# Loads, an operand sum and feed-forward buffers placed anew in a one-core encoder block

## The chip, the cores and the metric

The kernel runs on one core of a Trainium2 chip. The metric is the device time of one execution in microseconds; the time before is the median of three runs. All engine times below come from one profiled execution of the kernel before.

## The reference

One layer over x of 2048 tokens by 1024 features, all in float32:

```python
h = rms_norm(x, pre_mix_g)
proj = h @ w_in                      # attention q/k/v, RWKV r/k/v + low rank, two gates
y_a = chunk_band_attention(q, k, v, rel_bias)
y_b = rwkv7_time_mix(p_rwkv, ...)
merged = gate_a * (y_a @ proj_a) + gate_b * (y_b @ proj_b)
x = x + rms_norm(merged @ w_out, post_mix_g)
hf = rms_norm(x, pre_ffn_g)
u = square(relu(hf @ w_up)) @ w_down # w_up 1024 x 4096, w_down 4096 x 1024
x = x + rms_norm(u, post_ffn_g)
```

`rms_norm` divides a row by the root of its mean square and multiplies by a gain.

## The kernel before, in words

**Number format.** Each float32 operand of a large product is split into a rounded high part and the rest (`split`, lines 69 to 71: a cast on ScalarE, ACT in the profile, then a subtraction on VectorE, DVE). A product is three matmuls (`mm3`, line 73): high by high, high by low, low by high. Nearly every large operand therefore passes through ACT and DVE before TensorE (PE) may use it.

**Mixing.** The 2048 tokens are worked on in four groups (g = 0 to 3) of 512. For each group `run` (line 1378) calls `phase_rwkv`, `phase_attention` and `phase_merge`. At the end of `phase_attention` eight blocks of branch B (y_b @ proj_b, times its gate) are computed by `branch` (line 1007) and stored in DRAM as md. `phase_merge` (line 1019) then does:

- for i in 0 to 7 the branch-A block: loads mb (md, line 1031), th (the gate, line 1011) and wraw (proj_a, line 1013), 256 KB each; 12 matmuls into ps_p; then th is multiplied, mb added and the sum split into mh and ml. The blocks where i is above 2 also advance the generator `beside` by one step.
- the output projection, in two halves n of 512 columns. Each half has eight blocks k: a w_out load of 256 KB, a split, and 12 matmuls into ps_o (four token tiles by three). In the second half, after blocks 0, 2, 4 and 6, the generator `between` is advanced by one step.

**`beside`** is one of twenty operand sums (`combine`, line 1087) for the feed-forward part, which needs sums and differences of blocks of its operands: four loads of 256 KB into cmb, four DVE subtractions in place, each a step of the generator and kept in program order on DVE, and four stores. Loads and stores go through GpSimd's queue (POOL). One such sum belongs to each merge; `run` takes its first step, the loads, just before `phase_merge`.

**`between`** is the norm of the next group's input, `phase_norm` (line 282): it loads the gain g_pre (512 KB) and for each of four token tiles loads x (512 KB) through SyncE's queue (SP), squares and sums it on ACT, makes the root on POOL, multiplies on DVE (line 298), and transposes it in eight matmuls (`transpose_split`, line 118; pstr), with a cast and a subtraction for each four.

**Order.** A planner places the traced instructions on each engine's queue by its own timing model. A ready instruction can so come ahead of those traced before it. Each engine runs its queue in order. `keep_in_program_order` pins an instruction behind the one traced before it on its engine; `queue_behind(a, b)` (line 83) places a behind b on a queue without waiting for b to finish. In the trace the transposes of the first token tile stand ahead of most of the output projection.

**Feed-forward part.** Two halves of two groups each. `phase_up` (line 1140) computes seven combinations of the hidden layer for sixteen pairs of blocks: five or seven products (ps_u) per pair, with operands from w_up (wraw split by `parts` into a1, s12, s3, s4) and from the combined h (tiles t4, b22, t2, t3, t1, each high and low). For the first eight pairs the first two products are made ahead, with the buffers a1, s12, s3 in turn. The hidden values pass `hidden` (an addition, Relu, Square) and go to DRAM as xd. `phase_down` (line 1258) runs 56 steps s; each loads an xd block and a w_down (or combined wd) block of 512 KB, splits both into one operand tile fop (16 KB in each partition; `operands`, line 1282), and does 24 matmuls into ps_dn. Operands are made two steps ahead. `final` (line 1324) adds up squares, normalizes, adds the residual and stores.

**Memory.** Pools on the left grow up, those with side="right" grow down, both as a stack: a pool opened later lies further in, over whatever an earlier closed pool had there. With reuse_waits="tile" a tile waits only for the tiles whose bytes it takes. The pools raw (four 4 KB tiles), cb and z (two 16 KB buffers) live through the whole feed-forward part; z holds the tiles z and X in the up phase and fop in the down phase.

Of the kernel before, what the change touches and what calls it, by code (L numbers as in the profile page):

```python
# [18 lines left out]
P = 128  # L19
D = 1024  # L20
# [30 lines left out]
class Block:  # L51
# [17 lines left out]
    def split(self, hi, lo, src):  # L69
        self.nc.scalar.copy(hi, src)  # L70
        self.nc.vector.tensor_tensor(lo, src, hi.bitcast(F32), ALU.subtract)  # L71

# [45 lines left out]
    def transpose_split(self, pt, src, hi, lo, tok):  # L118

        nc = self.nc  # L120
        for h in range(2):
            ps = pt.tile([P, 4, P], F32, tag="tr", name="pstr")
            for j in range(4):
                k = h * 4 + j
                nc.tensor.transpose(ps[:, j], src[:, k * P : (k + 1) * P], self.ident)
# [166 lines left out]
    def norm_tile(self, sp, pt, x, gt, hi, lo, tok, ahead=2):  # L292
# [6 lines left out]
        self.transpose_split(pt, xn, hi, lo, tok)  # L299
# [719 lines left out]
    def phase_merge(self, g, o, op, between, beside):  # L1019

        tc, nc, a = self.tc, self.nc, self.a
        with ExitStack() as ctx:
# [6 lines left out]
            for i in range(KB):  # L1029
# [5 lines left out]
                if i > 2:  # L1035
                    advance(beside, 1)
            self.yctx.close()
            for n in range(2):
                ps = [po.tile([P, 512], F32, tag="o", name="ps_o") for _ in range(GT)]
                for k in range(KB):  # L1040
# [7 lines left out]
                    if n == 1 and k % 2 == 0:  # L1048
                        advance(between, 1)
# [51 lines left out]
    def combinations(self, half):  # L1101
# [4 lines left out]
        for k in range(KH):  # L1106
            src = (g0[:, k], g1[:, k], g0[:, KH + k], g1[:, KH + k])
            yield lambda b, src=src, k=k: self.combine(
                b, lambda i, t: dma(t, src[i]), lambda i, t: dma(self.td[half][:, i, k], t)
            )  # L1110

    def down_combinations(self):
# [3 lines left out]
        for i in range(FF // P // 2):  # L1116
            yield lambda b, i=i: self.combine(
                b, lambda c, t: dma(t, rows[i, c // 2, c % 2]), lambda c, t: dma(self.wd[c][i // 2][:, i % 2], t)
            )

# [19 lines left out]
    def phase_up(self, half, zp, rp, cb, pn, early):  # L1140
# [6 lines left out]
        with ExitStack() as ctx:  # L1147
            e = ctx.enter_context
            tb = e(tc.tile_pool(name="ht", bufs=1, reuse_waits="tile"))
            up = e(tc.tile_pool(name="up", bufs=1, reuse_waits="tile"))  # L1150
            sp = e(tc.tile_pool(name="ops", bufs=1, side="right", reuse_waits="tile"))
            bh, bl = self.b1
            B11, B21 = (bh[:, lo4], bl[:, lo4]), (bh[:, hi4], bl[:, hi4])
            z = zp.tile([P, early, G], F32, tag="z", name="z")
            X = zp.tile([P, 7, G], F32, tag="z", name="X")
            T = {
                n: [tb.tile([P, KH, G], F32R, name=n + x) for x in "hl"] for n in ("t4", "b22", "t2", "t3", "t1")
# [24 lines left out]
            def parts(src, tag, n):  # L1182
                hl = [sp.tile([P, n, P], F32R, tag=tag + x, name=tag + x) for x in "hl"]
# [74 lines left out]
    def phase_down(self, half, zp, rp, cb, pn, beside_of):  # L1258
# [213 lines left out]
```

## Time and profile before

| | us |
|---|---|
| median of three runs | 3354.83 (3352.9 to 3360.96) |
| the profiled execution | 3351.23 |
| its span in the profile | 3349.5 |
| PE busy | 3205.5 (96%) |
| DVE busy | 2245.0 (67%) |
| ACT busy | 1581.6 (47%) |
| POOL busy | 605.0 (18%) |
| DMA over the span | 592.56 MB, mean 177 GB/s |

The profiled execution's time holds the span and what lies around it. Rows of the timeline read: start, duration, engine, line, operation, tile written <- tiles read, shapes, count, and in brackets how long the engine was idle before and what ended that. SPq and POOLq are the queues that issue DMAs. A row of the windows reads: stretch, its length, busy time of the engine with its instructions in parentheses, the granted TensorE clock, the share of the 16 DMA engines' time, GB/s. PEld rows are TensorE's weight loads, which overlap its matmuls.

### The profile page before, as it was taken

The page shows a single profiled execution, that of the slowest core. Times are in us where ns is not written, and L with a number is a line of the kernel's source. Part 1 is how long each engine was busy: PE and PEld are TensorE (multiplying, and loading weights), DVE is VectorE, ACT ScalarE, POOL GpSimd, SP SyncE. Part 2 cuts the span into 40 slices and gives each one's busy share as a digit, 9 for nine tenths or more (in the row PEclk, how much of TensorE's full clock was granted, in tenths as well). Part 3 has the DMA queues.
Part 4 walks back from the last instruction along what each step waited for, and adds up shares of the span by engine and source line. Part 5 has one row for each costly group of instructions (what it writes and reads, how often), then busy time and mean ns, then how long its engine had stood idle before and what let it go on. Part 6 is the DMA issues. An engine that isn't in the chain of part 4 may idle for free. (4 is left out here: it accounts for less than half of the span.)

```text
span 3349.5 us, 50328 instructions
## 1 busy us (share of the span) xinstructions
PE 3205.5 (96%) x18913; PEld 2602.6 (78%) x18913; DVE 2245.0 (67%) x3719; ACT 1581.6 (47%) x2575; POOL 605.0 (18%) x1109
## 2 busy tenths in 40 slices
PE   7999989999989999999999999999999999999998
PEld 5777768777878777777777787878788878787887
DVE  5775666786765875765876765777655757774465
ACT  3434634444644434654444654544543444454333
POOL 2222012222111222111222110122211112210000
PEclk9999999999999999999999999999999999999999
DMA  5335374247464236655326647654777875546665
GB/s 150 89 117 188 112 227 125 79 139 241 152 227 139 88 109 221 196 178 176 95 77 200 199 138 239 232 179 161 253 259 245 291 228 190 167 160 225 195 211 180
DMA packets 448668, 592.56 MB, mean 177 GB/s; under 512 B 26324, under 2 KB 313248, under 8 KB 448424
## 3 DMA queue, kind: packets, MB, share of 16 engines
q1 hardware_dynamic: 390184, 408.94, 39.4%
q0 software_dynamic: 49024, 163.61, 13.6%
q10 hardware_dynamic: 9216, 16.78, 1.4%
q8 instruction: 149, 2.44, 0.3%
q14 instruction: 95, 0.78, 0.1%
HBM read 425.37 MB, written 167.01 MB: 177 GB/s over the span
## 5 line engine op out<-in xcount | busy, mean ns | idle before, releaser
L1307 PE MATMUL ps_dn<-fop 128*128 128x512 f32 x2688 | 614.6, 390 | 8.6 <-ACT fop L70 5.2
L1307 PEld LDWEIGHTS ps_dn<-fop 128*128 128x128 f32 x2688 | 505.6, 188 | 115.6 <-ACT fop L70 6.1
L79 PE MATMUL psd<-hh,whi 128*128 128x512 f32 x1344 | 539.3, 401 | 10.0 <-ACT whi L70 7.5
L79 PE MATMUL psd<-hh,wlo 128*128 128x512 f32 x1344 | 538.2, 400 | 2.7 <-DVE wlo L71 2.6
L79 PE MATMUL psd<-hl,whi 128*128 128x512 f32 x1344 | 539.8, 402 | 0.0
L70 ACT CAST whi<-wraw 128x1024 fp32r<-128x1024 f32 (+1 forms) x296 | 255.6, 864 | 546.5 <-PE psd L79 328.2
L71 DVE TENSOR_TENSOR wlo<-wraw,whi 128x1024 fp32r<-128x1024 f32 (+1 forms) x296 | 292.6, 989 | 238.5 <-ACT whi L70 206.2
L79 PEld LDWEIGHTS psd<-hh,whi 128*128 128x128 f32 x1344 | 255.1, 190 | 61.1 <-ACT whi L70 8.3
L79 PEld LDWEIGHTS psd<-hh,wlo 128*128 128x128 f32 x1344 | 255.1, 190 | 54.9 <-DVE wlo L71 5.2
L79 PEld LDWEIGHTS psd<-hl,whi 128*128 128x128 f32 x1344 | 255.0, 190 | 49.0
L71 DVE TENSOR_TENSOR fop<-xraw,fop 128x1024 fp32r<-128x1024 f32 x112 | 137.1, 1224 | 182.7 <-ACT fop L70 182.0
L70 ACT CAST fop<-xraw 128x1024 fp32r<-128x1024 f32 x112 | 117.7, 1051 | 262.8 <-PE ps_dn L1307 204.3
L1194 POOL DMA_DIRECT2D xd<-X x192 | 103.8, 541 | 395.2 <-ACT X L1191 341.0
L71 DVE TENSOR_TENSOR fop<-wdraw,fop 128x1024 fp32r<-128x1024 f32 x112 | 136.6, 1220 | 19.8 <-ACT fop L70 19.3
L70 ACT CAST fop<-wdraw 128x1024 fp32r<-128x1024 f32 x112 | 117.6, 1050 | 31.3 <-DMA wdraw<-in_w_down_dram 22.4
L880 DVE CUSTOM_DVE_ANT_0 sc<-bias,ps_s 128x640 f32<-128x640 f32 (+4 forms) x128 | 93.9, 734 | 55.9 <-PE ps_pt L891 39.6
L79 PE MATMUL ps_p<-yh,whi 128*128 128x512 f32 x256 | 103.4, 410 | 17.1 <-ACT whi L70 16.8
L70 ACT CAST s12h<-s 128x1024 fp32r<-128x1024 f32 x32 | 33.7, 1054 | 166.5 <-PE ps_u L79 166.5
L896 DVE TENSOR_TENSOR PTl<-ps_pt,PTh 128x640 fp32r<-128x640 f32 (+4 forms) x128 | 94.4, 738 | 26.4 <-ACT PTh L895 25.7
L885 ACT ACTIVATE sc<-sc,mn 128x640 f32<-128x640 f32 (+4 forms) x128 | 97.6, 763 | 26.8 <-DVE mn L880 26.5
L895 ACT CAST PTh<-ps_pt 128x640 fp32r<-128x640 f32 (+4 forms) x128 | 79.9, 624 | 52.8 <-PE ps_pt L891 50.4
L79 PE MATMUL ps_p<-yh,wlo 128*128 128x512 f32 x256 | 103.8, 406 | 1.0 <-DVE wlo L71 1.0
(368 smaller groups left out, 6861.5 us busy)
## 6 DMA issues: line engine op xcount, KB each, us to landing
wraw<-in_w_in_dram SPq DMA_DIRECT2D x168, 512.0 KB
xraw<-xd SPq DMA_DIRECT2D x112, 512.0 KB
xd<-X POOLq DMA_DIRECT2D x192, 256.0 KB, 5.1
wraw<-in_w_up_dram SPq DMA_DIRECT2D x80, 512.0 KB
wdraw<-wd SPq DMA_DIRECT2D x64, 512.0 KB
wdraw<-in_w_down_dram SPq DMA_DIRECT2D x48, 512.0 KB
gd<-gate ACTq DMA_DIRECT2D x64, 256.0 KB
cmb<-in_w_down_dram POOLq DMA_DIRECT2D x64, 256.0 KB, 4.4
```

Of the source, the lines that this page charges most:

```text
L70: self.nc.scalar.copy(hi, src)
L71: self.nc.vector.tensor_tensor(lo, src, hi.bitcast(F32), ALU.subtract)
L79: mm.append(nc.tensor.matmul(ps, l, r, start=n == 0, stop=n == last).ins)
L880: nc.vector.tensor_tensor_reduce(sc[:, 0:n], bias[:, s0:640], pss[:, c0 : c0 + n], 1.0, 3.0e38, ALU.add, ALU.min, mn,)
L885: nc.scalar.activation(sc[:, 0:n], sc[:, 0:n], AF.Exp, scale=-1.0, bias=mn, accum_out=sm[:, col : col + 1])
L895: nc.scalar.copy(hv, pst[:, 0:nk])
L896: nc.vector.tensor_tensor(lv, pst[:, 0:nk], hv.bitcast(F32), ALU.subtract)
L1194: nc.gpsimd.dma_start(self.xd[q][i // 2][:, i % 2], src)
L1307: nc.tensor.matmul(ps, o[:, l, k, sl], o[:, r, k], start=start and n == 0, stop=stop and n == end)
```

## The change

In the merge:

- The operand sum's five steps move from the branch loop and from before it into the first half of the output projection, after blocks 0 (loads), 3, 4, 5 and 6 (subtractions, then stores). The loads go through SP's queue instead of POOL's and are pinned there.
- The next group's norm is a new generator, `next_norm`. Its first step, after block 2 of the first half, loads the first x tile, the gain and the second x tile, pinned on SP's queue. Its four other steps come after blocks 0, 2, 4 and 6 of the second half as before; the first transpose of each four is now pinned on PE's queue. x tiles 2 and 3 are loaded right behind the steps of tiles 0 and 1, pinned too.

In the feed-forward part:

- `phase_up` has a second pool on the right, ops2, for s3 and s4 and a pad of 512 bytes; a1 and s12 stay in ops. The order of the tiles t1 and t2 in their pool is exchanged.
- In `phase_down` the pool ffo (x, gain, small tiles) is opened before ffb and ring instead of after them, with a small pad; in the second half, where ffb has nothing to hold, it gets a pad of 20,992 bytes.
- fop tiles alternate between z and ring with each step, instead of two steps in z and two in ring.
- The last Relu of the up phase is queued behind the second cast of step 1's operand on ACT.

The diff, cut where a description above says it all:

```diff
     def split(self, hi, lo, src):
-        self.nc.scalar.copy(hi, src)
+        high = self.nc.scalar.copy(hi, src)
         self.nc.vector.tensor_tensor(lo, src, hi.bitcast(F32), ALU.subtract)
+        return high.ins
...
-    def transpose_split(self, pt, src, hi, lo, tok):
+    def transpose_split(self, pt, src, hi, lo, tok, pinned=False):
...
-                nc.tensor.transpose(ps[:, j], src[:, k * P : (k + 1) * P], self.ident)
+                mm = nc.tensor.transpose(ps[:, j], src[:, k * P : (k + 1) * P], self.ident)
+                if pinned and j == 0:
+                    self.tc.keep_in_program_order(mm)
...
+    def next_norm(self, g, sp, pt):
+
+        pin, dma = self.tc.keep_in_program_order, self.nc.sync.dma_start
+        gt, xs = sp.tile([P, D], F32, tag="gain", bufs=1, name="g_pre"), []
+
+        def load(t):
+            xs.append(sp.tile([P, D], F32, tag="x", bufs=2, name="x"))
+            pin(dma(xs[-1], self.a["x"][g * G + t * P : g * G + (t + 1) * P]))
+
+        load(0)
+        pin(dma(gt, self.a["pre_mix_g"][None, :].to_broadcast((P, D))))
+        load(1)
+        yield
+        self.h = self.alloc_h()
+        for t in range(GT):
+            self.norm_tile(sp, pt, xs[t], gt, *self.h, slice(t * P, (t + 1) * P), 2, True)
+            if t + 2 < GT:
+                load(t + 2)
+            yield
...
                 self.split(mh[:, i], ml[:, i], t)
-                if i > 2:
-                    advance(beside, 1)
...
-                    if n == 1 and k % 2 == 0:
+                    if n == 0 and k in (0, 3, 4, 5, 6):
+                        advance(beside, 1)
+                    if n == 0 and k == 2 or n == 1 and k % 2 == 0:
                         advance(between, 1)
...
+    def load_in_order(self, dst, src):
+        self.tc.keep_in_program_order(self.nc.sync.dma_start(dst, src))
...
+            late = e(tc.tile_pool(name="ops2", bufs=1, side="right", reuse_waits="tile"))
             sp = e(tc.tile_pool(name="ops", bufs=1, side="right", reuse_waits="tile"))
...
+            late.tile([P, 128], F32, tag="pad", bufs=1, name="pad")
...
-                n: [...] for n in ("t4", "b22", "t2", "t3", "t1")
+                n: [...] for n in ("t4", "b22", "t1", "t3", "t2")
...
-                hl = [sp.tile([P, n, P], F32R, tag=tag + x, name=tag + x) for x in "hl"]
+                pool = sp if tag in ("a1", "s12") else late
+                hl = [pool.tile([P, n, P], F32R, tag=tag + x, name=tag + x) for x in "hl"]
...
-                nc.scalar.activation(dst, dst, AF.Relu)
+                self.relu = nc.scalar.activation(dst, dst, AF.Relu).ins
...
+            op = e(tc.tile_pool(name="ffo", bufs=2, side="right", reuse_waits="tile"))
             bp = e(tc.tile_pool(name="ffb", bufs=2, side="right", reuse_waits="tile"))
             ring = e(tc.tile_pool(name="ring", bufs=2, side="right", reuse_waits="tile"))
-            op = e(tc.tile_pool(name="ffo", bufs=2, side="right", reuse_waits="tile"))
...
+            op.tile([P, 32], F32, tag="pad", bufs=1, name="pad")
+            if half:
+                bp.tile([P, 5248], F32, tag="pad", bufs=1, name="pad")
...
-                t = (zp, ring)[s % 4 // 2].tile([P, 4, 2, G], F32R, tag=("z", "op")[s % 4 // 2], name="fop")
+                t = (zp, ring)[s % 2].tile([P, 4, 2, G], F32R, tag=("z", "op")[s % 2], name="fop")
...
-                self.split(t[:, 2], t[:, 3], wr)
+                high = self.split(t[:, 2], t[:, 3], wr)
+                if s == 1:
+                    self.queue_behind(self.relu, high)
...
-                    beside = next(sums)([b[:, i] for i in range(4)])
-                    advance(beside, 1)
-                    self.phase_merge(g, o, op, self.phase_norm(g + 1, sp, pt) if g + 1 < self.NG else iter(()), beside)
+                    beside = next(sums)([b[:, i] for i in range(4)], self.load_in_order)
+                    self.phase_merge(g, o, op, self.next_norm(g + 1, sp, pt) if g + 1 < self.NG else iter(()), beside)
```

The two generators that make operand sums take the load function as an argument (`get=dma`), so that only the sum beside a merge loads through SP.

More of the change, by code (lines that the diff above doesn't have):

```diff
@@ L290, in phase_norm, with norm_tile @@
             yield
-    def norm_tile(self, sp, pt, x, gt, hi, lo, tok, ahead=2):
+    def next_norm(self, g, sp, pt):
[14 more added lines that the diff above has]
+            yield
+    def norm_tile(self, sp, pt, x, gt, hi, lo, tok, ahead=2, pinned=False):
         nc = self.nc
@@ L298, in norm_tile @@
         nc.vector.scalar_tensor_tensor(xn, x, r, gt, op0=ALU.mult, op1=ALU.mult)
-        self.transpose_split(pt, xn, hi, lo, tok)
+        self.transpose_split(pt, xn, hi, lo, tok, pinned)
     def mix(self, g, blk, out):
@@ L1107, in combinations @@
             src = (g0[:, k], g1[:, k], g0[:, KH + k], g1[:, KH + k])
-            yield lambda b, src=src, k=k: self.combine(
-                b, lambda i, t: dma(t, src[i]), lambda i, t: dma(self.td[half][:, i, k], t)
+            yield lambda b, get=dma, src=src, k=k: self.combine(
+                b, lambda i, t: get(t, src[i]), lambda i, t: dma(self.td[half][:, i, k], t)
             )
@@ L1156, in phase_up @@
             T = {
-                n: [tb.tile([P, KH, G], F32R, name=n + x) for x in "hl"] for n in ("t4", "b22", "t2", "t3", "t1")
+                n: [tb.tile([P, KH, G], F32R, name=n + x) for x in "hl"] for n in ("t4", "b22", "t1", "t3", "t2")
             }
```

4 lines of the change are left out of this document (2 added, 2 removed).

## The prediction

> **What bounds the kernel now.** I read the page first, then who waited for whom on TensorE, then each idle stretch of TensorE in the timeline, then the busy time by stage.
>
> ```profile
> span 3349.5 us, 50328 instructions
> ```
>
> TensorE is busy for 96% of this span, so only its idle time, and the time in which it runs slowly after idling, can be won. Who ends its waits:
>
> ```profile
> PE ps_p L79 <- ACT whi L70: 16.8, 7, 4.7
> PE pstr L125 <- DVE xn L298: 14.5, 4, 10.1
> ...
> PE ps_dn L1307 <- ACT fop L70: 5.2, 2, 3.2
> ...
> PE ps_o L1045 <- ACT whi L70: 3.9, 4, 1.3
> ...
> PE ps_u L79 <- ACT a1h L70: 3.4, 1, 3.4
> PE ps_dn L1307 <- DVE fop L71: 3.3, 3, 2.1
> PE ps_u L79 <- DVE a1l L71: 3.2, 1, 3.2
> ```
>
> Columns: total us, times, longest. The branch products (ps_p) wait for their split weights, the next group's transposes (pstr) for the normed rows (10.1 us of that row is the kernel's start, which the change leaves alone; 4.4 are its three merges), and the feed-forward part waits for its first operands. All of these lie at places that the diff touches. In the windows around them:
>
> ```profile
> 441.00:480.00 39.00, 29.81 (x121) 1.00 0.87 288
> 480.00:498.00 18.00, 18.00 (x81) 1.00 0.46 146
> 971.00:1002.00 31.00, 23.77 (x97) 0.94 0.90 309
> 1494.00:1523.00 29.00, 23.49 (x95) 0.94 0.92 312
> 2012.00:2034.00 22.00, 18.96 (x75) 0.92 0.90 295
> 2034.00:2056.00 22.00, 20.31 (x85) 1.00 0.90 281
> 2397.00:2409.00 12.00, 6.74 (x20) 0.74 0.91 311
> 2710.00:2724.00 14.00, 7.44 (x19) 0.63 0.82 260
> 3036.00:3044.00 8.00, 5.67 (x24) 1.00 0.97 337
> ```
>
> Columns: length, TensorE busy (instructions), granted clock, DMA share, GB/s. Rows 1, 3 and 4 are the last branch blocks and the first output-projection blocks of groups 0, 1 and 2, row 2 the rest of the first half in group 0; rows 5 and 6 the same and most of the first half in group 3; 7 and 9 the starts of the two down phases; 8 the start of the second up phase. The undisturbed pace is in the chain that ended last:
>
> ```profile
> 3039.76 290.46 PE ps_dn L1307 x1280
> ```
>
> 290.46 / 1280 = 0.227 us per matmul. A row counts about 1.7 matmuls that straddle an edge, as row 2 shows (79.3 x 0.227 = 18.0). What each window lost is its length less (count - 1.7) x 0.227: 11.9, 9.4 and 7.8 us in groups 0 to 2 (29.1; the eight short transposes in each are counted as matmuls, so this is a little low), 5.4 + 3.1 = 8.5 in group 3, and 7.8, 10.1 and 2.9 in the feed-forward part (20.8). 58.4 us, 1.7%, is all that the change can reach.
>
> **Part 1: what leaves the branch stretch of groups 0 to 2.** How a weight comes late there (group 1):
>
> ```profile
> 967.87 0.38 SPq L63 DMA_DIRECT2D wraw<-in_proj_a_dram  x1
> ...
> 978.31 0.62 ACT L70 CAST whi<-wraw 128x512 fp32r<-128x512 f32 x1 [6.32 <-DMA wraw<-in_proj_a_dram]
> 978.98 0.50 PE L79 MATMUL ps_p<-yh,whi 128*128 128x512 f32 x1 [4.69 <-ACT whi L70]
> ```
>
> A 256 KB load needed 10.4 us. In the same microseconds stood these:
>
> ```profile
> cmb<-in_w_down_dram POOLq DMA_DIRECT2D x4, 256.0 KB, 8.3
> ...
> g_post<-in_post_mix_g_dram SPq DMA_DIRECT2D x1, 512.0 KB
> g_pre<-in_pre_mix_g_dram SPq DMA_DIRECT2D x1, 512.0 KB
> ```
>
> The change moves the four cmb loads (1.05 MB), their four stores (1.05), g_pre (0.52) and two x tiles (1.05) behind the start of the output projection: 3.67 MB, 11.9 us at the 309 GB/s of that window. g_post stays. Of the 9.6 MB that the window moved (31 us x 309) 5.9 remain, for 21.6 us of matmuls: 273 GB/s, under the 309 that it reached; groups 0 and 2 come to 279 and 254 in the same way. So the stretch goes from short of bandwidth to just fed. What is late next is a single weight load in the stretch's own queue, since 273 of 309 leaves little room; group 0 lost time before any cmb load was issued. I leave 3.5, 2.5 and 2.5 us (between 0 and half of the losses, 14.5 in all), and take 20.6 off.
>
> The four subtractions leave the branch loop too:
>
> ```profile
> L1094 DVE TENSOR_TENSOR cmb<-cmb x96: 678/682/694, 263.8 to 2639.3; 128x512 f32<-128x512 f32 x96
> ```
>
> 4 x 0.68 = 2.7 us of VectorE per merge, hidden before and after, since VectorE is not the bound of either stretch; uncovered they would cost 2.7. They keep their place in VectorE's queue, now behind the weight splits of the first half; if cmb were not there, the next low weight parts queued behind would wait, and TensorE for them. They come three blocks after the loads, 8 us.
>
> **Part 2: what the first half of the output projection takes on.** Its eight blocks (8 x 12 x 0.227 = 21.8 us) load 2.1 MB of w_out and now 3.67 MB more: 265 GB/s on average, against 146 in row 2. But on SP's queue the cmb loads are pinned behind the first w_out load, and x, g_pre, x behind the third; the w_out loads that follow come after 1.05 and 1.57 MB, 3.4 and 5.1 us at 309 GB/s. Two raw buffers let a weight be issued two blocks (5.4 us) ahead, and a quarter-megabyte load is there in about 3:
>
> ```profile
> DMA to landing us min/median/max: 2.4/3.1/7.5
> ```
>
> (this is of the th tiles, the same size, mostly in the branch stretch). That leaves 2.4 us of cover for each wave: 1.0 + 2.7 = 3.7 us if nothing else gives, 8.5 if there is no cover, and less than nothing if today's waits of ps_o (3.9 us in all) go as well. I take 2 us for each of three groups, nearer to the covered end because the waits there are short even with x loads and cmb stores beside them. The pinned transposes, now at blocks 0, 2, 4 and 6 of the second half, stand where rows were loaded 20 us before; their 4.4 us of waiting is within the 29.1. Groups 0 to 2 in sum: 20.6 - 6 = 14.6 off.
>
> **Group 3** has no next norm. Its branch stretch loses the cmb traffic (5.4 us of loss down to 2), but its first half already loses 3.1 at 281 GB/s, since the feed-forward part's first loads run there, and gets cmb on top: 5. 1.5 us off (0 to 5).
>
> **Part 3: the feed-forward buffers.** Steps 0 and 1 of a down phase both take their operand from the pool z, whose other buffer holds X until its last store. So step 1 waited for step 0's matmuls:
>
> ```profile
> 3036.26 1.04 ACT L70 CAST fop<-xraw 128x1024 fp32r<-128x1024 f32 x1 [1.15 <-PE ps_dn L1307]
> ```
>
> Now step 1 takes a ring buffer. By the sizes in the code the new order puts the first ring tile exactly over t3l and t2h and the second over t2l, s12, s4 and q: t3's last product has three products behind it, 3 x 12 x 0.227 = 8.2 us, and step 0 gives 5.4 more. Two casts and two subtractions (2 x 1.04 + 2 x 1.22 = 4.5 us) fit. The last Relu is queued behind the second cast on ScalarE; nothing on TensorE waits for it, as its results are loaded many steps later, so its price is 0, or 2 us if ScalarE stood still for the cast's data. Late next is step 2, which takes the z buffer when step 0's matmuls end and has step 1's 5.4 us for the same 4.5. Losses 7.8 and 2.9 go to 1.5 and 0.4.
>
> At the start of the second up phase:
>
> ```profile
> 2712.59 1.03 ACT L70 CAST a1h<-wraw 128x1024 fp32r<-128x1024 f32 x1
> ...
> 2713.67 0.79 PE L79 MATMUL ps_u<-bh,a1h 128*128 128x512 f32 x1 [3.37 <-ACT a1h L70]
> ...
> 2716.34 1.41 DVE L1340 SCALAR_TENSOR_TENSOR u<-u,rs_r,x1r 128x512 f32<-128x512 f32 x2
> 2717.66 1.22 DVE L71 TENSOR_TENSOR a1l<-wraw,a1h 128x1024 fp32r<-128x1024 f32 x1
> ```
>
> The cast starts after the last down matmul because a1 lies under the ring's last operand, and the low part queues behind the closing norm (u) on VectorE. In the new order a1 and s12 (16 KB) lie wholly under the pool ffb, free long before, and only s3 under ffo, in use until the closing norm ends. So the first two blocks (2 x 24 x 0.227 = 10.9 us of matmuls) can start at once, and s3 is late next: today the norm ends at 2717.75, 7.5 us after the last matmul (2713.67 - 3.37 = 2710.30), and s3's split takes 1.03 + 1.22. 10.1 goes to 2.5 (0 to 8, as the planner must still issue these splits early). Part 3: 20.8 - 4.4 = 16.4 off.
>
> One row against a rule. After the second idle stretch of the first down phase:
>
> ```profile
> 2404.43 5.06 PE L1307 MATMUL ps_dn<-fop 128*128 128x512 f32 x11 [2.11 <-DVE fop L71]
> ```
>
> Eleven matmuls take 5.06 us instead of 2.5: a 2.1 us stall cost 2.5 more, and this is in the 7.8. The Trainium skill (TensorE: Matmul & The Clock Gate, Part 1) has the clock fall only after an idle window of some 3.4 us; by that alone this loss would be 5.3 and the sum 2.5 smaller. The row decides.
>
> **Sum**: 14.6 + 1.5 + 16.4 = 32.5 us. The profiled execution took 3351.2 us (span 3349.5 and 1.7 around it) and would take 3318.7. The median shown is 3354.83, 3.6 above it, which I carry over: 3322.3.
>
> **The rivals.**
> First, the moved loads stop the first half. Without any cover, 2.62 MB ahead of w_out on one queue cost 8.5 us in three groups and 3.4 in group 3: 28.9 in place of 6, so that the sum is 20.6 - 25.5 + 1.5 - 3.4 + 16.4 = 9.6 off, 3345.2. For it: SP's queue is in order and the 10.4 us row. Against it: the two buffers ahead and the short ps_o waits. The Trainium skill (DMA: Bandwidth & Descriptors, Queues, rings and completion order) says that an engine takes descriptors of one ring in order and alternates between rows, which speaks for this rival: cmb comes from POOL's row, where it shared, to SP's, where it goes first. No row here shows the two side by side. Chance 0.14.
>
> Second, the new placement doesn't do what it says: the planner issues the operands of step 1 and of a1 as late as before. Then only 14.6 + 1.5 = 16.1 come off, 3338.7. For it: the a1l split queues behind the norm by the planner's choice, not by memory alone. Against: the cast of step 1 starts at once when step 0's matmuls end, that of a1 2.3 us after the last one; both follow their memory. Chance 0.16.
>
> Third, slower: the pinned transposes. They now hold their place in TensorE's queue, and the third and fourth x tiles are loaded only when the norm frees a buffer. If each came late, six waits (two in each of three groups) would stop TensorE with the whole projection behind. It decides from 32.5 / 6 = 5.4 us each; at the 10.4 us landing less 3.1, 7.3 us, it would be 44 us, 3366. Against: the second half gets no load that it hasn't today, and even row 2, with x loads in it, has a DMA share of 0.46. Chance 0.04.
>
> **How the numbers follow.** Forecast 0.66, rivals 0.14, 0.16 and 0.04. About 0.3% (10 us) is what a measurement here can tell from no change. The forecast and the second rival are faster by more than that; the first stands at the edge and I halve it: faster 0.89, same 0.08, slower 0.03. The range reaches down by the lower bounds (all six first-half us and some 9 us of the remainders gained too: 3307) and up over the second rival to 3340; the first and third are mostly left out.
>
> **What would show it.** In the changed profile: no cmb, g_pre or x load before the last two branch blocks; ps_p waits for whi under 6 us in total (16.8 now); pstr waits only at the start; the DMA share in the first half up from row 2's 0.46 to 0.8 or more, with ps_o waits of up to 6 us; ps_dn waits near 1 us and no half-clock matmuls at the down phases' starts; a1h cast before the last down matmul. It is wrong if ps_o's waits grow beyond 20 us, if a1 or fop rows stand where they stood, or if losses appear where the diff has nothing, through a new order.

## The result and the profile after

The kernel after takes 3326.35 us (median of four runs, 3323.82 to 3329.85) beside 3356.33 us (3352.9 to 3360.96) of the kernel before on the same chip: a ratio of 0.9911, 95% interval 0.9893 to 0.9928. By the medians 30.0 us are gone; 32.5 were forecast. The profiled execution took 3325.37 us, 25.9 less than that of before (3351.23), which was faster than the four executions timed here.

From here on "before" and "after" are the two kernels, and each ratio is to the kernel before, run beside it on the same chip. Parentheses hold the range of the times and the 95% interval of a ratio. Who ended TensorE's waits (total us, times, longest):

```profile
PE ps_o L1066 <- ACT whi L70: 8.5, 9, 2.0
PE ps_o L1066 <- DVE wlo L71: 4.8, 7, 1.1
...
PE ps_p L80 <- ACT whi L70: 3.6, 5, 1.2
...
PE ps_dn L1341 <- DVE fop L71: 1.5, 2, 0.8
...
PE ps_dn L1341 <- ACT fop L70: 0.8, 1, 0.8
```

The branch products' waits fell from 16.8 to 3.6 us, those at the down phases' starts from 8.5 to 2.3, and those of the second up phase for a1 are gone. In their place stand the waits of the output projection: 8.5 + 4.8 + 1.7 (for the product o) = 15.0 us where there were 4.8. In the windows, the last branch blocks and the first half for groups 0, 1, 2 and 3 in turn (length, TensorE busy and instructions, clock, DMA share, GB/s):

```profile
438.00:467.00 29.00, 27.05 (x112) 1.00 0.89 269
467.00:498.00 31.00, 27.38 (x112) 0.94 0.68 226
959.00:987.00 28.00, 27.14 (x115) 1.00 0.92 281
987.00:1016.00 29.00, 26.10 (x117) 1.00 0.71 234
1474.00:1501.00 27.00, 26.63 (x113) 1.00 0.89 278
1501.00:1531.00 30.00, 25.74 (x111) 1.00 0.68 230
2000.00:2022.00 22.00, 20.73 (x89) 1.00 0.87 281
2022.00:2050.00 28.00, 24.59 (x99) 1.00 0.95 285
```

By the prediction's own rule (length less (count - 1.7) x 0.227) the branch stretches of groups 0 to 2 lose 4.0, 2.3 and 1.7 us, as forecast (3.5, 2.5, 2.5). The first halves lose 6.0, 2.8 and 5.2 where 2 each was forecast: 14.0 for 6. And they do so at a mean DMA share of 0.68 to 0.71, not at the 0.8 or more that was expected. The mean hides two states. In group 1, around the two places where TensorE waits:

```profile
990.00:993.00 3.00, 1.85 (x8) 1.00 0.99 367
...
996.00:999.00 3.00, 2.08 (x8) 1.00 0.02 7
```

The transfer engines were full while the bunched loads went through and idle a few microseconds later. Over the whole half they had room, so the order of the loads has to be looked at. Group 3 loses 2.2 + 5.9 = 8.1 (7 forecast). What happens in a first half, in the timeline of group 1 (SP's queue, then ACT, DVE and PE; in brackets the idle time and what ended it):

```profile
981.58 0.33 SPq L63 DMA_DIRECT2D wraw<-in_w_out_dram  x1
...
982.55 1.84 SPq L1145 DMA_DIRECT2D cmb<-in_w_down_dram  x4
984.50 2.55 SPq L63 DMA_DIRECT2D wraw<-in_w_out_dram  x2
987.09 0.42 SPq L302 DMA_DIRECT2D x<-in_x_dram  x1
987.57 0.42 SPq L305 DMA_DIRECT2D g_pre<-in_pre_mix_g_dram  x1
988.03 0.43 SPq L302 DMA_DIRECT2D x<-in_x_dram  x1
991.85 11.88 SPq L63 DMA_DIRECT2D wraw<-in_w_out_dram  x5
...
990.48 0.62 ACT L70 CAST whi<-wraw 128x512 fp32r<-128x512 f32 x1 [1.04 <-DMA wraw<-in_w_out_dram]
...
995.42 1.06 ACT L319 ACTIVATE xn<-x 128x1024 f32<-128x1024 f32 x1 [1.31 <-DMA x<-in_x_dram]
...
996.48 0.60 ACT L70 CAST whi<-wraw 128x512 fp32r<-128x512 f32 x1
...
997.52 1.28 DVE L321 SCALAR_TENSOR_TENSOR xn<-x,rs_r,g_pre 128x1024 f32<-128x1024 f32 x1 [1.16 <-POOL rs_r L107]
998.72 0.69 DVE L71 TENSOR_TENSOR wlo<-wraw,whi 128x512 fp32r<-128x512 f32 x1
...
991.15 1.20 PE L1066 MATMUL ps_o<-whi,mh 128*128 128x512 f32 x4 [1.51 <-ACT whi L70]
...
999.46 0.50 PE L1066 MATMUL ps_o<-wlo,mh 128*128 128x512 f32 x1 [1.13 <-DVE wlo L71]
```

Two things are to be seen. The second and third weight of w_out stand behind four cmb loads, and the fourth behind x, g_pre and x. And the norm's square (995.42, itself waiting for its x tile) stands on ScalarE ahead of a weight's cast, its product (997.52, waiting for POOL) on VectorE ahead of a weight's low part, for which TensorE then waits 1.13 us. With the blocks counted from 0, the longer stops stand at the same two places in groups 0, 1 and 2: at block 1, whose weight stands behind the cmb loads (1.61, 1.51 and 1.98 us), and at block 3, behind the norm's steps (0.65, 0.25 and nothing for the high part, 1.14, 1.13 and 1.13 for the low part).

In the feed-forward part, the start of the first down phase with the ScalarE row that made it late, the cast of a1, and the start of the second down phase:

```profile
2388.84 10.95 PE L1341 MATMUL ps_dn<-fop 128*128 128x512 f32 x47 [0.69 <-DVE fop L71]
2400.62 0.49 PE L1341 MATMUL ps_dn<-fop 128*128 128x512 f32 x1 [0.83 <-ACT fop L70]
2401.88 12.54 PE L1341 MATMUL ps_dn<-fop 128*128 128x512 f32 x47 [0.77 <-DVE fop L71]
...
2396.77 1.05 ACT L70 CAST fop<-xraw 128x1024 fp32r<-128x1024 f32 x1 [6.81 <-DMA xraw<-xd]
...
2675.69 1.05 ACT L70 CAST a1h<-wraw 128x1024 fp32r<-128x1024 f32 x1
...
3007.44 14.89 PE L1341 MATMUL ps_dn<-fop 128*128 128x512 f32 x65
```

Step 1 of the first down phase waits 0.69 us instead of 3.15 + 2.11; step 3, whose xd block landed late, waits 0.83 + 0.77, and the 47 matmuls behind it run at 12.54 / 47 = 0.267 us instead of 0.227. The cast of a1 is 20 us ahead of the last down matmul. The second down phase starts without a stop.

### The profile page after: what moved, and what is told of

It is laid out like the page before. It is cut to its first block, busy times and chain, and to the rows that moved or that the text cites. A ratio compares the mean times of both kernels' runs of the same rounds, so it can differ in the third digit from the quotient of the medians.

```text
span 3323.7 us, 50325 instructions
## 1 busy us (share of the span) xinstructions
PE 3198.8 (96%) x18913; PEld 2597.9 (78%) x18913; DVE 2248.2 (68%) x3719; ACT 1581.6 (48%) x2575; POOL 592.7 (18%) x1093
## 5 line engine op out<-in xcount | busy, mean ns | idle before, releaser
L80 PE MATMUL psd<-hh,whi 128*128 128x512 f32 x1344 | 540.1, 402 | 10.8 <-ACT whi L70 7.6
L1066 PE MATMUL ps_o<-whi,mh 128*128 128x512 f32 x256 | 98.8, 400 | 10.2 <-ACT whi L70 8.5
L1066 PE MATMUL ps_o<-wlo,mh 128*128 128x512 f32 x256 | 101.8, 398 | 4.9 <-DVE wlo L71 4.8
```

The source lines that it names most:

```text
L80: mm.append(nc.tensor.matmul(ps, l, r, start=n == 0, stop=n == last).ins)
L1066: nc.tensor.matmul(ps[t], l[:, k, ts], r[:, 0], start=k == 0 and j == 0, stop=k == KB - 1 and j == 2)
```

## The experiments

The theory after the result (A): the loads and the steps that came into the first half make w_out's weights late by their place on SP's, ScalarE's and VectorE's queues, not by their amount; the feed-forward part gained as forecast, by where its buffers lie. The rivals: the amount of data bounds the first half; or the feed-forward part gained by a new order of the planner.

For the merge the table takes from each kernel's profiled execution the first and last matmuls of the stages, and shows how much longer or shorter a stage is than before, summed over the four groups. In before, four matmuls of the projection stood ahead of the last branch block and eight transposes ahead of the rest of the first half in groups 0 to 2; so about 3 x 0.9 us of the shorter branch stretch come back in the first half, and as much in the second, as work that only moved. Runs e1, e6 and e7 have the merge of after, word for word, and e2 that of before. Among the four with after's merge the branch column differs by up to 4.7 us, the first halves by 2.3 and the last column by 6.3, which is how far one row may be trusted.

| us against before | branch products | first half | second half | all three |
|---|---|---|---|---|
| after | -30.3 | +18.9 | +3.6 | -7.8 |
| e1 merge alone | -33.6 | +16.8 | +3.4 | -13.4 |
| e6 (merge of after) | -28.9 | +18.5 | +3.2 | -7.1 |
| e7 (merge of after) | -32.4 | +19.1 | +3.2 | -10.1 |
| e2 (merge of before) | +3.2 | -0.5 | +1.6 | +4.3 |
| e3 sum in second half | -27.6 | +18.3 | +5.8 | -3.6 |
| e4 norm behind splits | -28.5 | +15.1 | +3.3 | -10.1 |
| e5 sum's loads on POOL | -16.6 | +17.1 | +2.7 | +3.2 |
| e9 loads one by one | -27.4 | +7.3 | +3.8 | -16.3 |
| e8 = e9 + e4 | -28.8 | +3.6 | +4.0 | -21.2 |
| e10 = e8, g_post later | -35.2 | +8.0 | +5.5 | -21.7 |
| e11 norm's loads apart | -29.4 | +11.4 | +3.5 | -14.5 |
| e12 sum's loads apart | -31.8 | +19.0 | +3.7 | -9.0 |

**The two parts by themselves.** e1 takes back every edit in the feed-forward part, e2 every edit in the merge.

> The kernel before with the merge part of the change alone (the sum and the norm's loads in the first half of the output projection), the feed-forward pools as before. The parts are separate theory: the four merges together are 6 to 9 us shorter (7.8 in the changed kernel's profile, from the first branch matmul to the last of the projection) and the feed-forward part stands where it stood; 3348 +- 3 us beside 3356. Rival, that the merge part is worth what I forecast (16 us) and the profiled run hid half of it: 3340.

> The kernel before with the feed-forward part of the change alone, the merge as before. Separate theory: the two down phases and the second up phase save 17 us as in the changed kernel's profile (first down phase 5, start of the second up phase 8, second down phase 3), 3339 +- 3 us. Rival, that a part of it comes from another order of the merge: under 12 us saved, 3344 or more. The ps_ht waits in the attention of groups 1 and 2 (5.2 us before, 1.4 after) should stay at 5 us here if they come from the merge's new order.

Measured: e1 3338.0 us (3331.93 to 3341.3), ratio 0.9938 (0.9923 to 0.9953); e2 3347.24 us (3338.12 to 3349.98), ratio 0.9960 (0.9946 to 0.9974). 0.62% and 0.40% make 1.02%, where both together gave 0.89% (0.72% to 1.07%): the two parts add up within what can be measured. In e2's trace the first down phase is 2.3 us shorter than before, the second up phase 7.7 and the second down phase 2.9, in sum 12.9; after itself has 4.8, 8.4 and 2.9. Both of these expectations missed, and in both the rival's number came nearer. The merge alone takes 20 us off the median, with merges 13.4 us shorter in its profile and not 6 to 9. The feed-forward part alone takes 10.8 us off, under the 12 of its rival. Its three phases are 12.9 us shorter, but its merges, unchanged in the program, are 4.3 us longer than before's. That lies within the scatter of the last column, so a dependence of the one part on the other isn't shown.

**The sum in the second half.** For groups 0 to 2:

```diff
-                    if n == 0 and k in (0, 3, 4, 5, 6):
+                    if n == (g + 1 < self.NG) and k in (0, 3, 4, 5, 6):
                         advance(beside, 1)
```

> The changed kernel with the operand sum (four loads, four subtractions, four stores) one half later, in the second half of the output projection of groups 0 to 2; group 3 as changed. Theory B, the w_out loads stand behind the moved loads: the wait for the second block of weights (1.5 us in group 1) goes, first halves lose 2 to 3 us less in each of three groups, 6 to 8 us in all against the changed kernel. Theory A, the norm's operations stand ahead of the weights' splits on ScalarE and VectorE: the first halves lose at most 1 us less each, 0 to 3 us in all. Either: no new loss in the second half, whose DMA share is 0.35.

Measured: 3329.65 us (3326.06 to 3332.48), ratio 0.9915 (0.99 to 0.9929), no different from after. The first halves, now without the sum's loads in three groups, are as long as in after (+18.3), and ps_o still waits 8.4 us for the high part and 4.4 for the low one. But the waits have moved. The stop at block 1, of which theory B spoke, is gone in groups 0 to 2; at block 3 the high part is now waited for 2.23, 0.80 and 1.83 us. Its cast stands there right behind the norm's second square, which waits for its x tile. So the norm's three loads with the steps that need them are enough to stop these halves by themselves, and what the sum's loads cost doesn't add to it. The second halves took 2.2 us more than in after, which neither theory had.

**The norm's first steps behind the splits.** The square and the product of tiles 0 and 1 are queued behind the weight splits of blocks 5 and 6, and 6 and 7:

```diff
+        if pinned and tok.start < 2 * P:
+            k = 5 + tok.start // P
+            self.queue_behind(sq.ins, self.parts_of[k][0])
+            self.queue_behind(mul.ins, self.parts_of[k + 1][1])
```

> The changed kernel with the Square and the multiplication of the first two token tiles queued behind the weight splits of blocks 5 and 6 (tile 0) and 6 and 7 (tile 1) of the first half; loads where the change put them. Theory A (norm ahead of the splits): the stalls in the middle of the first half (1.1 us in each of groups 0 to 2, more with the slow matmuls behind them in group 0) go, 4 to 6 us in all. Theory B (weights land late): the splits still wait for their loads, at most 1 us in all.

Measured: 3319.91 us (3318.37 to 3321.24), ratio 0.9885 (0.9869 to 0.9902). Who waits for the low part now:

```profile
PE ps_o L1074 <- DVE wlo L71: 2.5, 9, 0.6
```

2.5 us instead of 4.8, the longest 0.6 instead of 1.1, and the waits for the high part stay (8.1 in all). At block 3 they are now 0.94, 0.95 and 0.95 us, and the cast waits for its weight's load. So the norm's steps ahead of a split were one cost, some 2 to 4 us, and the smaller; theory A had 4 to 6, theory B 1 at most. The intervals of this run and of after overlap, so the trace carries this, not the time.

**Another queue for the sum's loads.**

```diff
-        self.tc.keep_in_program_order(self.nc.sync.dma_start(dst, src))
+        self.tc.keep_in_program_order(self.nc.gpsimd.dma_start(dst, src))
```

> The kernel after, but the operand sum's four loads, at their new place in the first half of the output projection, go through GpSimd's queue again (pinned there) instead of SP's. Theory A (what the first half loses comes from the sum's loads standing ahead of the w_out loads on SP's own queue): with them on another queue the weights overtake them, the waits of ps_o for the high part (8.5 us in the kernel after) fall by at least half, and the kernel is 3 to 6 us faster than the kernel after: a ratio of 0.990 or below beside 0.9911. Theory B (the waits come from the amount of data, 0.92 to 0.95 of the DMA time in the first blocks, and from the norm's own steps on ScalarE and VectorE): it doesn't matter which queue the sum's loads stand on: within 2 us of the kernel after, ps_o waits of 7 to 10 us for the high part.

Both theories miss. Measured: 3348.44 us (3341.36 to 3351.38), ratio 0.9962 (0.9948 to 0.9976), 17 us above after by the ratios. Group 1, POOL's queue and the weight cast behind it, and then the branch products' waits:

```profile
967.05 2.14 POOL L1145 DMA_DIRECT2D cmb<-in_w_down_dram  x4
...
976.67 0.62 ACT L70 CAST whi<-wraw 128x512 fp32r<-128x512 f32 x1 [5.42 <-DMA wraw<-in_proj_a_dram]
```

```profile
PE ps_p L80 <- ACT whi L70: 14.2, 4, 4.1
```

Pinned in the program behind the first w_out block, the loads were issued 26 us before the output projection began (992.93), right behind the last md store: nothing on POOL's queue waits for the weights. They are back in the branch stretch, and so are its waits (14.2 us; 16.8 before). So it is SP's queue, in which a load stands behind weight loads that wait for buffers, that moves the traffic at all. The same row shows the price of the traffic: 1.05 MB of sum's loads in a branch stretch cost 30.3 - 16.6 = 13.7 us over four groups (12 to 17 against the four rows with after's merge).

**Loads one by one.** e8 on top of e4, e9 on top of after: each load of the sum behind a block of its own (0 to 3), its subtractions behind blocks 4 to 7; the norm's three loads behind blocks 1, 3 and 5.

```diff
-                    if n == 0 and k in (0, 3, 4, 5, 6):
+                    if n == 0:
                         advance(beside, 1)
-                    if n == 0 and k == 2 or n == 1 and k % 2 == 0:
+                    if n == 0 and k in (1, 3, 5) or n == 1 and k % 2 == 0:
                         advance(between, 1)
```

> The kernel with the norm's first squares and products queued behind the weight splits (3319.9 us, ratio 0.9885), and on top of it the moved loads are issued one by one: one load of the sum behind each of the blocks 0 to 3 of the first half, the first x tile behind block 1, the gain behind 3, the second x tile behind 5; the sum's subtractions behind blocks 4 to 7. Theory A (bunches of 1 to 1.6 MB pinned ahead of the next weight on one queue make the weights late): no weight has more than 0.8 MB ahead of it, the waits of ps_o for the high part fall from 8.1 us to 3 or less, and the ratio goes to 0.986 to 0.9875. Theory B (the amount of data in these blocks is the limit, or the branch stretch and the first block): no change beyond 2 us, 0.988 to 0.989, ps_o waits of 6 to 9 us.

> The kernel after with the moved loads issued one by one as in the run before, but without queueing the norm's first squares and products behind the weight splits. Theory A (two separate costs in the first half: the bunched loads, about 8 us over the four groups, and the norm's steps ahead of a weight's split, 3 us): 3313 us or so, a ratio of 0.9875 (0.986 to 0.989), with ps_o waiting for the low part about 4.5 us in all and for the high part 1 us or less. Theory B (the norm's steps did harm only because the weights were late already): the same as with both, 0.985 to 0.986.

Measured: e8 3309.76 us (3308.07 to 3315.85), ratio 0.985 (0.9833 to 0.9867); e9 3314.63 us (3307.53 to 3318.39), ratio 0.9864 (0.9849 to 0.9878). The first halves fall from +18.9 to +7.3 (e9), and with the norm's steps queued behind the splits as well to +3.6 (e8), of which 2.7 only moved there. In e8, SP's queue in group 1, the windows of the first halves of groups 0, 1 and 3, and the waits that are left:

```profile
975.95 0.42 SPq L1156 DMA_DIRECT2D cmb<-in_w_down_dram  x1
976.77 0.33 SPq L63 DMA_DIRECT2D wraw<-in_w_out_dram  x1
977.16 0.42 SPq L1156 DMA_DIRECT2D cmb<-in_w_down_dram  x1
977.63 0.42 SPq L303 DMA_DIRECT2D x<-in_x_dram  x1
```

```profile
466.50:489.40 22.90, 22.45 (x97) 1.00 0.77 256
980.40:1003.50 23.10, 22.64 (x96) 1.00 0.79 263
...
2009.20:2033.60 24.40, 22.78 (x97) 1.00 1.00 305
```

```profile
PE ps_o L1076 <- DVE wlo L71: 2.8, 8, 0.8
```

The same data in the same half: DMA share 0.77 and 0.79 in groups 0 and 1, where it was 0.68 and 0.71, losses of 1.3 and 1.7 us, no wait for a high part among them. Even group 3, at a share of 1.00 and 305 GB/s, loses only 2.8. That settles it against the amount in the half; what counted was how much of it stood in one piece. Whether the norm's steps still cost anything on top can't be told by the times (the intervals of e8 and e9 overlap); the waits for the low part went from 3.8 in e9 to 2.8.

**Which of the two bunches.** e11 takes apart the norm's loads alone, e12 the sum's alone, both on top of after (the two lines of the diff above, one each).

> The kernel after, with only the next norm's loads issued apart (first x tile behind block 1 of the first half, gain behind 3, second x tile behind 5); the sum's four loads still go in one bunch behind block 0. Against the kernel after, the first halves of the four groups together shrank by 11.6 us when both bunches were broken up. Theory A (the bunch of the norm's loads, 1.57 MB, is the costly one, as the kernel with the sum in the second half waited as much): 7 to 9 us of these come from this edit, all in groups 0 to 2: a ratio of 0.988 to 0.989, group 3 unchanged. Theory B (the sum's bunch, 1.05 MB, is the costly one): within 2 us of the kernel after.

> The kernel after, with only the sum's four loads issued apart (behind blocks 0 to 3 of the first half, its subtractions behind 4 to 7); the norm's loads still go in one bunch of 1.57 MB behind block 2. Theory A (the norm's bunch is the costly one): 3 to 4 us off in the first halves, most of it in group 3, which has no norm (2.7 us there): a ratio of 0.990. Theory B (the sum's bunch is the costly one): 8 us or more off, 0.9885 or below.

Measured: e11 3317.13 to 3323.49 us in three runs (a fourth, of 16499 us, is not in the ratio), ratio 0.9885 (0.9869 to 0.9901); e12 3330.66 us (3323.25 to 3334.9), ratio 0.9919 (0.9905 to 0.9933). In e11 the first halves of groups 0 to 2 are 7.6 us shorter than in after (9.3 for 16.9; the other kernels with after's merge have 14.9 to 16.8, so 5.6 to 7.6) and that of group 3 as long (2.1 for 2.0). In e12 group 3's is 2.3 us shorter and the others are no shorter (19.3). The sums follow theory A, but the places of the stops say that it is not the whole account. In e11 the stops at block 3 are gone, those behind the norm's steps too, and those at block 1 stay: 2.38, 0.72 and 1.52 us. In e12 those at block 1 are gone, and at block 3 the high part is waited for 2.53, 1.32 and 2.43 us (the low part as in after). Group 0 of e11, then of e12 with the ScalarE rows ahead of the stop:

```profile
472.35 1.21 PE L1068 MATMUL ps_o<-whi,mh 128*128 128x512 f32 x4 [2.38 <-ACT whi L70]
```

```profile
476.40 1.06 ACT L319 ACTIVATE xn<-x 128x1024 f32<-128x1024 f32 x1 [1.84 <-DMA x<-in_x_dram]
...
477.46 0.60 ACT L70 CAST whi<-wraw 128x512 fp32r<-128x512 f32 x1
...
478.11 1.20 PE L1066 MATMUL ps_o<-whi,mh 128*128 128x512 f32 x4 [2.53 <-ACT whi L70]
```

So in groups 0 to 2 each bunch stops TensorE at a place of its own, the sum's at block 1, the norm's at block 3, there by way of the square that waits for its x tile and holds up a weight's cast. The waits don't add: with the first gone, the second is longer, and e12 gains nothing there. So e11's gain is the worth of that edit in this kernel, with the norm's steps in it, and not the price of 1.57 MB alone. In group 3, which has no norm, the sum's bunch costs by itself.

**The closing norm's gain leaves the branch stretch too.** On top of e8, g_post is loaded behind block 3 of the first half, the norm's three loads behind 1, 5 and 7.

> Both edits (loads one by one, the norm's first steps behind the splits: ratio 0.985), and the gain of the closing norm, g_post, 512 KB, leaves the branch stretch too: it is loaded behind block 3 of the first half, the next norm's gain behind 5 and the second x tile behind 7. Theory A (what is left in the branch stretch, ps_p waits of 5.0 us, is bandwidth): 0.52 of about 5.9 MB less there, 1.7 us at 309 GB/s in each of four groups, so 3 to 6 us off: 0.983 to 0.984, with ps_p waits of 3 us or less, and the first half still fed at some 290 GB/s. Theory B (the remainder is the first weight loads behind the attention's end, not bandwidth): within 2 us of the run without it, 0.9845 to 0.9855; if the first half overflows instead, ps_o's waits grow by 3 us or more and it is slower.

Measured: 3311.38 us (3311.07 to 3315.57), ratio 0.9856 (0.984 to 0.9872). In the branch stretch it did what bandwidth says, another 6.4 us in four groups (35.2 for 28.8), and the waits of ps_p for the high part are down from 5.0 to 0.4 us. But the first halves took 4.4 of it back and the second halves 1.5:

```profile
PE ps_o L1075 <- DVE o L1089: 4.1, 3, 1.4
```

The product o needs g_post; as that comes late, the banks of ps_o come free late (4.1 us; 0.8 in e8), and 2.5 us of waits for the high part are back, of which e8 has none. What theory A had for the stage came out, its time (0.983 to 0.984) did not: between e8's and e10's times no difference can be told.

**The feed-forward edits, one back at a time.** e6 has the operand tiles two in z and two in the ring again, and no Relu queued behind a cast; e7 opens the pools of the down phase in the old order, without pads.

```diff
-                t = (zp, ring)[s % 2].tile([P, 4, 2, G], F32R, tag=("z", "op")[s % 2], name="fop")
+                t = (zp, ring)[s % 4 // 2].tile([P, 4, 2, G], F32R, tag=("z", "op")[s % 4 // 2], name="fop")
```

> The kernel after, but the down phase's operand tiles lie two steps in z and two in the ring as before, and the last Relu isn't queued behind a cast. Theory A (step 1 waited for step 0's matmuls because both took a buffer of z): the two down starts get back their losses, 4.8 and 2.9 us between the kernels before and after: 3334 us (3331 to 3337), a ratio of 0.9934, and the second step's cast again starts at the end of step 0's matmuls. Theory B (the down starts gained because the pools were ordered anew): the time stays within 1.5 us of the kernel after, 0.9911.

> The kernel after, but the pools of the down phase are opened in the old order (the small tiles of the closing norm innermost, no pads), while fop tiles alternate and s3 and s4 stay in a second pool. Theory A (the second up phase began late because a1 lay under tiles that were in use to the end of the down phase): the start loss comes back, 3.5 us at the start and up to 8 in the whole phase: 3330 to 3335 us, a ratio of 0.9922 to 0.9937, with the cast of a1 after the last down matmul again. Theory B (the start of the up phase gained from s3 and s4 having a pool of their own, or from the planner's new order): within 1.5 us of the kernel after.

Measured: e6 3328.51 us (3326.74 to 3333.91), ratio 0.9905 (0.989 to 0.992); e7 3333.01 us (3328.48 to 3342.15), ratio 0.9919 (0.99 to 0.9939). Neither time can be told from after's, so the stages must decide (us against before):

| | first down | second up | second down |
|---|---|---|---|
| after | -4.8 | -8.4 | -2.9 |
| e6 | -4.2 | -6.9 | 0.0 |
| e7 | -5.2 | -0.6 | -2.9 |

The first column is the loosest: with the feed-forward part of after, word for word, the first down phase is 0.8 us (e5) to 5.3 us (e4) shorter than before. The last column stands at -2.9 in all of these runs.

e6 at both down starts, PE and the cast before it:

```profile
2387.48 23.92 PE L1339 MATMUL ps_dn<-fop 128*128 128x512 f32 x96 [3.10 <-ACT fop L70]
...
3013.56 1.20 PE L1339 MATMUL ps_dn<-fop 128*128 128x512 f32 x4 [2.08 <-ACT fop L70]
...
3011.52 1.04 ACT L70 CAST fop<-xraw 128x1024 fp32r<-128x1024 f32 x1 [1.14 <-PE ps_dn L1339]
```

At the second start the wait of before is back to the hundredth (2.08 us, the cast behind step 0's matmuls): the shared buffer was its cause. At the first start step 1 also waits again (3.10 us; 3.15 before), and yet the phase stays 4.2 us shorter than before. The second stop, 2.11 us, with the slow matmuls behind it, has not come back. In before, this stood between the low parts on VectorE:

```profile
2400.82 1.29 DVE L1069 SCALAR_TENSOR_TENSOR xr<-o_prev,rs_p,xr 128x1024 f32<-128x1024 f32 x1
```

In e6 it comes after them. That is the planner's new order; with which edit it came isn't shown. So theory A holds at the second down start, and at the first one it doesn't.

e7 at the start of the second up phase:

```profile
2693.42 1.03 ACT L70 CAST a1h<-wraw 128x1024 fp32r<-128x1024 f32 x1
...
2694.50 0.50 PE L80 MATMUL ps_u<-bh,a1h 128*128 128x512 f32 x1 [3.37 <-ACT a1h L70]
2699.76 0.80 PE L80 MATMUL ps_u<-bh,a1l 128*128 128x512 f32 x1 [4.06 <-DVE a1l L71]
```

The 3.37 us of before are back, and the wait for the low part behind the closing norm too: 7.8 of the 8.4 us. The order of the pools with its pads was the cause; the second pool for s3 and s4 alone gains next to nothing. The exchange of t1 and t2 and the Relu's place were not taken back by themselves.

## Why the prediction was nearly right

- **Part 1, the branch stretch: right.** Remainders 4.0, 2.3 and 1.7 us for 3.5, 2.5 and 2.5. It had 279, 273 and 254 GB/s for what remained; the windows show 269, 281 and 278. (Its 3.67 MB were a little too much: group 1's cmb loads were issued from 966.70 on, up to 4.3 us ahead of its window.) That traffic beside the weights costs there is shown by e5, which put 1.05 MB back on another queue and lost 13.7 us. e10 took 0.52 MB more out of each group and gained 6.4; as that load had stood on the weights' own queue, its place and its bytes can't be told apart.
- **Part 2, "I take 2 us for each of three groups": this term was mis-sized.** The first halves lose 6.0, 2.8 and 5.2 us, 14.0 for 6. The working ahead of the choice came nearer: 1.0 us behind the sum's bunch and 2.7 behind the norm's, 3.7 a group, for a measured 14.0 / 3 = 4.7. The argument that pulled it down, short ps_o waits before the change, came from halves in which nothing was pinned ahead of a weight. The two prices were not right one by one. The stop behind the sum's bunch is 1.7 us a group for 1.0. At block 3 the weight itself is late by 0.95 us a group for 2.7, once the norm's steps are out of its way (e4). That e11 gains 7.6 / 3 = 2.5 us a group is therefore no confirmation of the 2.7: the waits that it takes away at block 3 (0.9 us for the high part, 3.4 for the low) stand behind the norm's own steps on ScalarE and VectorE, which moved with its loads and of which the part didn't speak; e4 puts 2 to 4 us on them. Nor do the two prices add up, as e3 and e12 show.
- **Group 3: right in the sum** (8.1 for 7), with its second term at 5.9 for 5.
- **Part 3, 16.4 us: right in size**, 4.8 + 8.4 + 2.9 = 16.1 in the profiled runs (6.3, 7.6 and 2.5 were forecast, and the 4.8 lies near the upper end of 0.8 to 5.3). The causes named hold for the second up phase (e7) and the second down phase (e6). At the first down phase step 1 did start earlier, but step 3 was late then, and e6 has nearly the same gain without the alternation: a change of order that the forecast hadn't named did at least part of it, and the alternation's share isn't shown.
- **The rivals.** The first, that the moved loads stop the first half, is what happened in part: 14.0 us in groups 0 to 2, between the forecast's 6 and its 25.5. The second, that the placement does nothing, falls by the a1h row and by e7. The third, the pinned transposes, falls: after the kernel's start, one wait of 10.3 us, no transpose waits for a normed row.
- **Not in the sum:** the transposes of the operand sums' residual (ps_ht) wait 1.4 us instead of 5.2. e2 and e5 keep 5.2, so it comes with the move of the sum's loads to SP's queue.
- **The sum.** The profiled runs differ by 25.9 us: 7.8 in the merges (16.1 forecast), 16.1 in the three stages of part 3, 1.5 in the first up phase, 0.7 before and between the merges, less 0.3 at the end. The medians differ by 30.0, nearer to the 32.5. Of the 4 us between the two counts, the merges are a candidate (the same code gives 13.4 in e1), and so is the stretch between the merges of groups 2 and 3, which is 5.2 us longer in after's profiled run and only 0.1 in e4's. A total that agrees to 2.5 us is partly luck: the first halves were 8 us worse than forecast, and what made up for part of it lies outside the sum.

## What to carry to other kernels

A queue with buffers behind it is a delay line: a load pinned behind weight loads that wait for buffers moves to another stage, and the same load pinned on an idle queue runs ahead to where it was (17 us between the two here). What is moved that way should come in pieces no larger than what the next weight's lead covers: the same bytes cost 11.6 us more in two bunches than one by one. Waits in one stage need not add: taking one bunch apart won 7.5 us in the first halves, taking the other apart nothing, and both together 11.6. Moving a load moves its consumers as well; look at what they stand ahead of on the engines that feed the critical one.

## What the runs showed of the hardware

A short stop of TensorE may be followed by slow matmuls or may not. In after, two stops of 0.83 and 0.77 us, 1.3 us apart, left 47 matmuls that took 12.54 us. In e8, a single stop of 1.50 us, nearly as long as the two together, is followed by none:

```profile
2375.36 10.99 PE L1352 MATMUL ps_dn<-fop 128*128 128x512 f32 x47 [1.50 <-DVE fop L71]
```

As many matmuls in 10.99 us, 0.234 each. The granted clock was 0.85 in after's stretch (2400.6 to 2412 us) and 1.00 in e8's (2375 to 2386). The Trainium skill (TensorE: Matmul & The Clock Gate, Part 1) has the clock fall after an idle window of some 3.4 us; the row of after doesn't agree, as none of its stops is near that. The prediction's row from before speaks less plainly than it was taken to: its stop of 2.11 us came 1.2 us after one of 3.15. Spells of this kind fall at other places from run to run: with the same stop of 1.14 us in it, block 3 of group 0 took 5.79 us in after and 4.27 in e1. What decides isn't shown here. So a loss of 3 us in one stage had to be read from that stage's first and last matmul, and not from the total.
